# Row sums of squares by transposing and reducing instead of multiplying by ones, in a two-layer decoder trunk

## The chip, the cores and the metric

The kernel runs on one core of a Trainium2 chip. The metric is the time of one execution on the device in microseconds (us). Before the change it is 1353.64 us, the median of three runs (1351.68 to 1353.88).

A core has a matrix engine (TensorE, PE in the profile; its weight loads are listed apart as PEld), three engines for elementwise work (VectorE or DVE, ScalarE or ACT, GpSimd or POOL), and a queue engine that starts transfers (SyncE or SP). Matrix products are written to PSUM, which this kernel uses as eight banks of 128x512 float32 values; the other working memory is SBUF. Each engine has its own list of instructions and waits in it where an input or a buffer isn't ready.

## The reference

Two layers act on 512 tokens of width 1024, in float32. Layer 0 mixes tokens by four retention heads and four mLSTM heads, layer 1 by sparse attention. Each layer then has a gated MLP with a short convolution, and an embedding that is normed, gated and added. What matters here are the norms:

```python
def rms_norm(x, g):
    xf = x.astype(jnp.float32)
    y = xf * lax.rsqrt(jnp.mean(xf * xf, axis=-1, keepdims=True) + EPS)
    return (y * g.astype(jnp.float32)).astype(x.dtype)
...
    ret = rms_norm(ret, ret_g.reshape(R_HEADS, R_DV)).reshape(B, T, -1) * jax.nn.silu(rg)
...
    mlstm = jax.nn.sigmoid(mo) * rms_norm(hm, m_g.reshape(M_HEADS, M_DV)).reshape(B, T, -1)
```

Each needs, for every token, the sum of squares over the features. There are eight such norms over the full width (two mixers, two MLPs, two embeddings, two gates) and one for each of the eight heads of layer 0. The norms of queries and keys in layer 1 are computed in another way and aren't touched.

## The kernel before

The residual `h` lies transposed: eight tiles of 128 features by 512 tokens. Every float32 matrix is split into a high and a low part (`split`, L136 on ScalarE and L137 mostly on VectorE), and a product is made of three (`mm3`, L176 to L178): high by high, high by low, low by high. A weight tile is loaded by SyncE (`wr`), split into `wh` and `wl` with three buffers each, and used.

Since features lie along partitions, a sum over features has two steps. First, `acc_square` squares each of the eight tiles on ScalarE (L229, L232) and adds them up into one tile `acc` of 128x512 on GpSimd and VectorE (L234). Then `norm_sum` must add along the partitions and have one number for each token: for each of the four blocks `j` of 128 tokens it multiplies the block, as the stationary operand, by two columns of ones (L299). The result for 128 tokens stands in two equal columns of a PSUM bank, and L301 takes every second one and scales it. Tokens are now along partitions, four columns `v`. `rsqrt` (L215 to L221) gets the inverse root by three Newton steps on VectorE. `norm_cast` brings it back along the free axis with `spread`, which transposes four broadcast columns on TensorE (L307), and ScalarE copies that to `rb` (L312). `rb` multiplies what comes out of the products, so the products themselves don't wait for the norm.

In layer 0 the output `num` of each head is squared on ScalarE (`sq`, 128 features by 512 tokens), and `square_sums` (L510, L511) adds it up in the same manner into the columns `hd::4` of a 16-column tile, with a bank of kind "b" for each head.

PSUM banks are of three kinds, "a" (4), "b" (3) and "o" (1). `norm_sum` uses the "o" bank. The gate stage (`ple_gate`) runs its products through the four "a" banks; the first of them are freed only when L1592 has multiplied them by `rb`.

The order of the instructions on each engine is not the order of the source. A scheduler simulates the program with its own costs of instructions and writes the order out, so another form of the sums also moves other instructions.

Of the kernel before, what the change touches and what calls it, by code (L numbers as in the profile page):

```python
# [16 lines left out]
ALU = mybir.AluOpType  # L17
AX = mybir.AxisListType.X
PSUM = bass.MemoryType.PSUM

P = 128
T = 512
NTT = T // P
D = 1024
# [4 lines left out]
EPS = 1e-6  # L29
# [34 lines left out]
class Trunk:  # L64
# [226 lines left out]
    def norm_scale(self, n):  # L291
        self.norm_sum(n)
        self.norm_cast(n)

    def norm_sum(self, n):
        nc = self.nc
        ps = self.ps("o")
        for j in range(NTT):
            nc.tensor.matmul(ps[:, 2 * j : 2 * j + 2], n.acc[:, j * P : (j + 1) * P], self.ones[:, 0:2], start=True, stop=True)  # L299
        v = self.small(4)  # L300
        nc.vector.tensor_scalar(v, ps[:, 0:8:2], 1.0 / D, EPS, ALU.mult, ALU.add)  # L301
        n.r = self.rsqrt(v, 4)

    def spread(self, cols):
# [58 lines left out]
    def ab_mixer(self):  # L363
        nc, I, tc = self.nc, self.I, self.tc
        with ExitStack() as ctx:
# [84 lines left out]
            def ret_probs(banks):  # L450
                s = s_tile()
                for b, (c0, c1) in zip(banks, PARTS3):
                    self.split(s[:, 0, c0:c1], s[:, 1, c0:c1], b[:, 0 : c1 - c0])
                for i in range(NTT):
                    d = s[:, :, OFF[i] : OFF[i] + P]
                    nc.gpsimd.affine_select(d, d, pattern=[[0, 2], [1, P]], compare_op=ALU.is_ge, fill=0.0, base=0, channel_multiplier=-1)
                return s
# [16 lines left out]
            def lstm_probs(banks, e):  # L474
                main, rest = e
                s = s_tile()
                for b, (c0, c1) in zip(banks, PARTS3):
                    x = rest if c0 == 1024 else main[:, c0:c1]
                    nc.vector.tensor_tensor(x, b[:, 0 : c1 - c0], x, ALU.mult)
                    self.split(s[:, 0, c0:c1], s[:, 1, c0:c1], x)  # L480
                return s
# [23 lines left out]
                return sq  # L505

            def square_sums(hd, sq, ss):
                pss = self.ps("b")
                for j in range(NTT):
                    nc.tensor.matmul(pss[:, 2 * j : 2 * j + 2], sq[:, j * P : (j + 1) * P], self.ones[:, 0:2], start=True, stop=True)  # L510
                nc.vector.tensor_copy(ss[:, hd::4], pss[:, 0:8:2])  # L511


            def gate_sum(src):
# [49 lines left out]
            n = Norm()  # L564
# [42 lines left out]
            for idx in (0, 2, 1, 3):  # L607
                ps = pm[idx] if idx in pm else self.ws(I["w_mqk"][idx], n)
# [12 lines left out]
            def ret_out(hd, s, g):  # L621
                num = attend(hd, s, rv)
                gated(num, g, C_ABG + hd, ru[hd])
                return square(num)

            banks = pair_scores(rqk, 0, ("a", "b", "a"))
            ss = [ret_probs(b) for b in banks]
# [8 lines left out]
            sq = [ret_out(hd, ss[hd], gs[hd]) for hd in range(2)]  # L636
# [3 lines left out]
            ss = [ret_probs(b) for b in banks]  # L640
# [4 lines left out]
            for hd in range(2):  # L645
                square_sums(hd, sq[hd], rss)
            sq = [ret_out(2 + x, ss[x], g) for x, g in enumerate((g2, g3))]
# [6 lines left out]
            for hd in range(2):  # L654
                square_sums(2 + hd, sq[hd], rss)
# [18 lines left out]
            for c in range(2):  # L674
                self.cycle = ("b",)
                ro += [finish(ru, rr, 2 * c + x) for x in range(2)]
                gs = [gate_sum(I["w_mo"][2 * c])]

                with self.behind(nc.tensor):
                    banks = pair_scores(mqk, c, ("a", "a", "b"))  # L680
                ss = [lstm_probs(banks[0], es[2 * c])]
                nc.scalar.activation(gs[0], gs[0], AF.Sigmoid)
                ss.append(lstm_probs(banks[1], es[2 * c + 1]))
                gs.append(gate_tile(I["w_mo"][2 * c + 1], AF.Sigmoid))
                while mq:
                    square_sums(*mq.pop(0), mss)
                if c:
                    add_sums(0)
                both_sums = [key_sums(es[2 * c + x]) for x in range(2)]
                for x in range(2):  # L690
                    hd = 2 * c + x
                    num = attend(hd, ss[x], mv)
                    gated(num, gs[x], C_ABG + 4 + hd, mu[hd])
                    mq.append((hd, square(num)))
                sums = sums + both_sums if c else both_sums
# [1035 lines left out]
```

## Time and profile before

| | |
|---|---|
| three timed runs | 1351.68, 1353.64, 1353.88 us |
| the profiled execution | 1351.2 us, of which 1349.1 us from the first to the last instruction (the span) |
| TensorE | busy 1331.1 us, 99% of the span |
| VectorE | busy 1015.9 us, 75% |
| ScalarE | busy 735.7 us, 55% |
| GpSimd | busy 402.8 us, 30% |
| granted TensorE clock | 0.999 in the mean |

Times in the profile count from the start of the span. A row of the timeline has the start, the duration, the engine, the line, the operation, what it writes and reads, the shape and how many were merged; in brackets stands how long the engine was idle before it, and what ended that. Matrix products overlap their neighbours, so a row's duration is longer than the step from one start to the next. A row of the groups by line has the total busy time and the mean of one in ns, and then the idle time ahead of the group. The eight norm sums start at 31, 246, 470, 600, 646, 954, 1180 and 1310 us, the head sums stand in pairs at 108, 119, 170 and 180 us.

### The profile page before, as it was taken

To read this page: it belongs to the slowest core of one execution; us is meant where nothing else is said; L and a number is where in the kernel's file an instruction comes from. 1 tells how busy PE (TensorE), PEld (TensorE's weight loads), DVE (VectorE), ACT (ScalarE), POOL (GpSimd) and SP (SyncE) were. 2 spreads that over 40 slices of the span, in tenths; PEclk is the share of its full clock that TensorE was granted. 3 is DMA by queue.
4 is the path that set the end of the run, shared out by engine and by line. 5 is a ranking of instruction groups with operands and counts; after the bars stand their busy time and mean duration, and the time that the engine had idled before them with its cause. 6 is when DMAs were issued, how large, how long until landed. Compare 5 with 4: busy or idle time off the path is not lost. (4 is left out here: it accounts for less than half of the span.)

```text
span 1349.1 us, 21058 instructions
## 1 busy us (share of the span) xinstructions
PE 1331.1 (99%) x7782; PEld 1152.5 (85%) x7782; DVE 1015.9 (75%) x1638; ACT 735.7 (55%) x1301; POOL 402.8 (30%) x414
## 2 busy tenths in 40 slices
PE   9999999999999999999999999999999999999998
PEld 7888888888999999888788888888787999999887
DVE  6775867697888877678777878766797888877675
ACT  5357525454555555345466888674454555554342
POOL 3356432132111100331422887572232111110320
PEclk9999999999999999999999999999999999999999
DMA  6522355226666653433243231113225666653331
GB/s 239 161 98 94 110 141 182 88 90 179 166 174 176 167 132 91 129 113 118 82 156 110 82 95 52 32 52 98 90 90 172 167 174 174 167 135 90 133 96 63
DMA packets 68590, 167.23 MB, mean 124 GB/s; under 512 B 8068, under 2 KB 12804, under 8 KB 68488
## 3 DMA queue, kind: packets, MB, share of 16 engines
q1 hardware_dynamic: 59560, 150.02, 34.9%
q0 software_dynamic: 8640, 15.73, 7.0%
q8 instruction: 61, 1.00, 0.3%
q14 instruction: 41, 0.34, 0.1%
q10 hardware_dynamic: 288, 0.14, 0.0%
HBM read 146.71 MB, written 7.35 MB: 114 GB/s over the span
## 5 line engine op out<-in xcount | busy, mean ns | idle before, releaser
L136 ACT ACTIVATE wh<-wr 128x1024 fp32r<-128x1024 f32 (+2 forms) x186 | 190.7, 1028 | 216.6 <-PE ps L177 155.2
L137 DVE TENSOR_TENSOR wl<-wr,wh 128x1024 fp32r<-128x1024 f32 (+2 forms) x169 | 211.1, 1250 | 71.9 <-ACT wh L136 70.4
L176 PE MATMUL ps<-y,wh 128*128 128x512 f32 (+1 forms) x648 | 225.0, 351 | 1.0 <-ACT y L136 0.9
L177 PE MATMUL ps<-y,wh 128*128 128x512 f32 (+1 forms) x648 | 225.6, 349 | 0.0
L178 PE MATMUL ps<-y,wl 128*128 128x512 f32 (+1 forms) x648 | 224.2, 348 | 0.0
L176 PE MATMUL ps<-g,wh 128*128 128x512 f32 x380 | 148.3, 390 | 0.0
L177 PE MATMUL ps<-g,wh 128*128 128x512 f32 x380 | 148.3, 390 | 0.0
L178 PE MATMUL ps<-g,wl 128*128 128x512 f32 x380 | 148.0, 389 | 0.0
L176 PEld LDWEIGHTS ps<-y,wh 128*128 128x128 f32 x648 | 122.6, 189 | 18.4 <-ACT y L136 1.3
L177 PEld LDWEIGHTS ps<-y,wh 128*128 128x128 f32 x648 | 122.8, 190 | 15.6
L178 PEld LDWEIGHTS ps<-y,wl 128*128 128x128 f32 x648 | 122.8, 189 | 15.3
L234 POOL TENSOR_TENSOR acc<-acc,sc 128x512 f32<-128x512 f32 x36 | 58.1, 1615 | 128.6 <-ACT sc L232 127.6
L1437 POOL DMA_DIRECT2D es<-in_w_up_dram x30 | 26.3, 896 | 228.9 <-DVE sc L1397 107.9
L1078 POOL TENSOR_SCALAR pr<-pr,sm,gate 128x512 f32<-128x512 f32 (+3 forms) x128 | 77.0, 623 | 26.3 <-DVE sm L1076 21.6
L1503 DVE TENSOR_TENSOR hp<-hp,ps 128x512 f32<-128x512 f32 x96 | 65.3, 682 | 25.4 <-PE ps L178 25.4
L178 PEld LDWEIGHTS ps<-g,wl 128*128 128x128 f32 x380 | 71.4, 188 | 14.9
L176 PEld LDWEIGHTS ps<-g,wh 128*128 128x128 f32 x380 | 71.5, 188 | 14.0
L177 PEld LDWEIGHTS ps<-g,wh 128*128 128x128 f32 x380 | 71.5, 188 | 13.8
L1067 ACT ACTIVATE pr<-ps,nmx 128x512 f32<-128x512 f32 (+3 forms) x128 | 68.0, 539 | 12.8 <-DVE nmx L1065 6.9
L1430 POOL DMA_DIRECT2D ep<-ep x30 | 26.6, 912 | 160.7 <-DVE a L1475 51.2
L1470 ACT ACTIVATE sc<-ps 128x256 f32<-128x256 f32 x120 | 45.5, 379 | 52.4 <-PE ps L178 50.4
L176 PE MATMUL ps<-y,gh 128*128 128x256 f32 x240 | 68.5, 285 | 2.1 <-ACT sc L1470 2.1
(378 smaller groups left out, 3585.2 us busy)
## 6 DMA issues: line engine op xcount, KB each, us to landing
wr<-in_w_up_dram SPq DMA_DIRECT2D x58, 512.0 KB, 3.5
wr<-in_w_down_dram SPq DMA_DIRECT2D x64, 256.0 KB, 3.0
ep<-in_w_up_dram SPq DMA_DIRECT2D x30, 512.0 KB, 6.0
wr<-in_w_plg_dram SPq DMA_DIRECT2D x16, 512.0 KB, 3.5
es<-in_w_up_dram SPq DMA_DIRECT2D x30, 256.0 KB, 3.0
es<-in_w_up_dram POOLq DMA_DIRECT2D x30, 256.0 KB, 6.4
ep<-ep POOLq DMA_DIRECT2D x30, 256.0 KB, 3.6
wr<-in_w_down_dram SPq DMA_DIRECT2D x32, 192.0 KB, 2.5
```

The costliest lines, as they stand in the source:

```text
L136: self.nc.scalar.activation(hi, src, AF.Copy)
L137: (eng or self.nc.vector).tensor_tensor(lo, src, hi.bitcast(F32), ALU.subtract)
L176: mm(out, ah, bh, start=first, stop=False, **kw)
L177: mm(out, ah, bl, start=False, stop=False, **kw)
L178: mm(out, al, bh, start=False, stop=last, **kw)
L234: eng.tensor_tensor(n.acc, n.acc, sq, ALU.add)
L1067: nc.scalar.activation(pr[:, b], s[:, b], AF.Exp, bias=nmx[:, b : b + 1], accum_out=sm[:, bs[b] : bs[b] + 1])
L1078: nc.gpsimd.tensor_scalar(prs[b], prs[b], sm[:, b : b + 1], gate[:, j, hd, 1 + b : 2 + b], ALU.mult, ALU.mult)
L1430: nc.gpsimd.dma_start(me.two[:, :T], me.two[:, T:], accum_op=ALU.add)
L1437: nc.gpsimd.dma_start(me.s3, I["w_up"][i, me.f][:, :T], accum_op=ALU.add)
L1470: copy = lambda out, ps: nc.scalar.activation(out, ps, AF.Copy)
L1503: nc.vector.tensor_tensor(self.h[m], self.h[m], ps, ALU.add)
```

## The change

A new helper `token_sums` transposes the four blocks of 128x128 on TensorE into one bank, so that tokens are along partitions and features along the free axis, and VectorE adds up the 128 values of each block (`tensor_reduce` over the last axis, 128x512 to 128x4). `norm_sum` calls it, and then scales the four columns with an instruction of its own. `square_sums` calls it in place of products and copy.

```diff
+    def token_sums(self, out, src, ps):
+        for j in range(NTT):
+            self.nc.tensor.transpose(ps[:, j * P : (j + 1) * P], src[:, j * P : (j + 1) * P], self.ident)
+        self.nc.vector.tensor_reduce(out, ps.rearrange("p (j d) -> p j d", j=NTT), AX, ALU.add)
+
     def norm_sum(self, n):
         nc = self.nc
         ps = self.ps("o")
-        for j in range(NTT):
-            nc.tensor.matmul(ps[:, 2 * j : 2 * j + 2], n.acc[:, j * P : (j + 1) * P], self.ones[:, 0:2], start=True, stop=True)
         v = self.small(4)
-        nc.vector.tensor_scalar(v, ps[:, 0:8:2], 1.0 / D, EPS, ALU.mult, ALU.add)
+        self.token_sums(v, n.acc, ps)
+        nc.vector.tensor_scalar(v, v, 1.0 / D, EPS, ALU.mult, ALU.add)
         n.r = self.rsqrt(v, 4)
...
             def square_sums(hd, sq, ss):
-                pss = self.ps("b")
-                for j in range(NTT):
-                    nc.tensor.matmul(pss[:, 2 * j : 2 * j + 2], sq[:, j * P : (j + 1) * P], self.ones[:, 0:2], start=True, stop=True)
-                nc.vector.tensor_copy(ss[:, hd::4], pss[:, 0:8:2])
+                self.token_sums(ss[:, hd::4], sq, self.ps("b"))
```

In the order of the changed kernel, lines up to 293 keep their numbers, L301 becomes L305, `spread` is L311 and L312 becomes L316; lines behind `square_sums` move up by one.

VectorE at the norm of the first MLP, before (`acc` holds the squares, `ps` the sums, `wl` are low parts of weights):

```order
L234 TENSOR_TENSOR acc_2152<-acc_2152,sc_2194 128x512
L137 TENSOR_TENSOR wl_2332<-wr_2330,wh_2331 128x1024
L301 TENSOR_SCALAR tiny_2264<-ps_2259 128x4
L137 TENSOR_TENSOR wl_2403<-wr_2401,wh_2402 128x1024
L215 TENSOR_SCALAR tiny_2267<-tiny_2264 128x4
L216 TENSOR_SCALAR tiny_2266<-tiny_2267 128x4
```

and in the changed kernel:

```order
L234 TENSOR_TENSOR acc_2153<-acc_2153,sc_2195 128x512
L137 TENSOR_TENSOR wl_2334<-wr_2332,wh_2333 128x1024
L298 TENSOR_REDUCE tiny_2261<-ps_2260 128x4
L137 TENSOR_TENSOR wl_2405<-wr_2403,wh_2404 128x1024
L305 TENSOR_SCALAR tiny_2261<-tiny_2261 128x4
L215 TENSOR_SCALAR tiny_2269<-tiny_2261 128x4
L216 TENSOR_SCALAR tiny_2268<-tiny_2269 128x4
```

The reduction stands where the scaling stood, and the scaling now follows the weight split; nothing else moved there.

TensorE in the gate stage of layer 0, before, from the spread (L307) to the first product of the next output bank (`ps_5973`; the products of L176 to L178 for one bank are 24):

```order
L307 MATMUL ps_5876<-ident,tiny_5862 128x128 x4
L177 MATMUL ps_5936<-y_5764,wh_5930 128x512
L178 MATMUL ps_5936<-y_5763,wl_5931 128x512
L176 MATMUL ps_5936<-y_5770,wh_5930 128x512
L177 MATMUL ps_5936<-y_5771,wh_5930 128x512
L178 MATMUL ps_5936<-y_5770,wl_5931 128x512
L176 MATMUL ps_5936<-y_5777,wh_5930 128x512
L177 MATMUL ps_5936<-y_5778,wh_5930 128x512
L178 MATMUL ps_5936<-y_5777,wl_5931 128x512
L176 MATMUL ps_5936<-y_5784,wh_5930 128x512
L177 MATMUL ps_5936<-y_5785,wh_5930 128x512
L178 MATMUL ps_5936<-y_5784,wl_5931 128x512
```

and in the changed kernel (`ps_5977` is the next bank):

```order
L178 MATMUL ps_5940<-y_5773,wl_5935 128x512
L311 MATMUL ps_5880<-ident,tiny_5866 128x128 x4
L176 MATMUL ps_5940<-y_5780,wh_5934 128x512
L177 MATMUL ps_5940<-y_5781,wh_5934 128x512
L178 MATMUL ps_5940<-y_5780,wl_5935 128x512
L176 MATMUL ps_5940<-y_5787,wh_5934 128x512
L177 MATMUL ps_5940<-y_5788,wh_5934 128x512
L178 MATMUL ps_5940<-y_5787,wl_5935 128x512
L176 MATMUL ps_5977<-y_5739,wh_5971 128x512
```

The spread moved back by five products: 6 of them now lie between it and the next bank, where there were 11. The last gate stage has the same move, the first norm moves its spread by four products and the layer-1 mixer by three.

ScalarE at the start of the layer-1 mixer, before (`wh` are high parts of weights, `rb` the spread norm):

```order
L136 ACTIVATE wh_6380<-wr_6379 128x1024
L136 ACTIVATE wh_6427<-wr_6426 128x1024
L312 ACTIVATE rb_6307<-ps_6308 128x512
L136 ACTIVATE wh_6458<-wr_6457 128x1024
L199 ACTIVATE sc_6340<-ps_6323 64x512
```

and in the changed kernel:

```order
L136 ACTIVATE wh_6385<-wr_6384 128x1024
L136 ACTIVATE wh_6432<-wr_6431 128x1024
L136 ACTIVATE wh_6463<-wr_6462 128x1024
L316 ACTIVATE rb_6312<-ps_6313 128x512
L199 ACTIVATE sc_6345<-ps_6328 64x512
```

One more weight copy now stands ahead of `rb`. On VectorE the split of that weight moved ahead of the first work with `rb` in the same way.

## The prediction

> **What bounds the kernel now.** I read the page's busy shares and slices first, then TensorE's waits, then single stretches of the timeline around the operations that change.
>
> ```profile
> PE 1331.1 (99%) x7782; PEld 1152.5 (85%) x7782; DVE 1015.9 (75%) x1638; ACT 735.7 (55%) x1301; POOL 402.8 (30%) x414
> ...
> PE   9999999999999999999999999999999999999998
> ```
>
> TensorE (PE) works through 99% of the 1349.1 us and is full in every slice. VectorE (DVE) has a quarter of the span free on average. So the first question for each edit is whether it shortens PE's own instruction stream, and the second is where PE already waits, since a gain ahead of such a wait is lost in it.
>
> ```profile
> PE ps L176 <- ACT wh L136: 2.9, 3, 1.2
> ...
> PE ps L177 <- DVE wl L137: 1.5, 1, 1.5
> ...
> PE ps L299 <- DVE acc L234: 0.8, 1, 0.8
> ```
>
> These are the longest of PE's waits for ScalarE and for VectorE, and the only one at a line that changes (us in total, times, longest). They are short, and none is a wait for a sum; the last is a sum that waits for its input.
>
> **PE: what is removed and added.** Sixteen groups change: eight norm sums (L299) and eight head sums (L510), each of four 128-column blocks.
>
> ```profile
> L299 PE MATMUL ps<-ones,acc x64: 164/251/252, 31.1 to 1310.6; 128*128 128x2 f32 x64
> ...
> L510 PE MATMUL ps<-ones,sc x64: 164/251/252, 108.5 to 181.7; 128*128 128x2 f32 x64
> ...
> L307 PE MATMUL ps<-ident,tiny x64: 271/273/289, 40.7 to 1319.5; 128*128 128x128 f32 x64
> ...
> L988 PE MATMUL ps<-ident,y x64: 272/273/298, 717.5 to 835.5; 128*128 128x128 f32 x64
> ```
>
> L299 issues 8 x 4 = 32 products and leaves 64 records: a product of float32 with the ones is two passes, each with a weight load, however few columns it has. L307, the helper `spread`, issues 16 x 4 = 64 transposes and leaves 64 records, and so does L988 (16 heads x 4), whose input is ordinary data as in the change. So the records fall from 128 to 64. The records overlap, so I take the cost of a group from the starts of its neighbours, the neighbours' own steps (0.23 us each) taken off:
>
> ```profile
> 246.19 0.39 PE L178 MATMUL ps<-g,wl 128*128 128x512 f32 x1
> 246.42 0.95 PE L299 MATMUL ps<-ones,acc 128*128 128x2 f32 x8
> 247.23 0.49 PE L176 MATMUL ps<-fh,wh 128*128 128x512 f32 x1
> 247.55 0.40 PE L177 MATMUL ps<-fh,wh 128*128 128x512 f32 x1
> ...
> 252.59 0.39 PE L178 MATMUL ps<-g,wl 128*128 128x512 f32 x1
> 252.81 0.60 PE L307 MATMUL ps<-ident,tiny 128*128 128x128 f32 x4
> 253.17 0.48 PE L176 MATMUL ps<-fh,wh 128*128 128x512 f32 x1
> 253.48 0.39 PE L177 MATMUL ps<-fh,wh 128*128 128x512 f32 x1
> ```
>
> A norm sum: 247.55 - 246.19 - 2 x 0.23 = 0.90 us. Four transposes: 253.48 - 252.59 - 0.46 = 0.43, say 0.44. Two head sums one after the other:
>
> ```profile
> 108.32 0.39 PE L177 MATMUL ps<-s,v 128*128 128x512 f32 x1
> 108.55 1.84 PE L510 MATMUL ps<-ones,sc 128*128 128x2 f32 x16
> 110.25 0.48 PE L178 MATMUL ps<-s,v 128*128 128x512 f32 x1
> 110.56 0.33 PE L176 MATMUL ps<-s,v 128*128 128x384 f32 x1
> ```
>
> 110.56 - 108.32 - 0.46 = 1.78, so 0.89 each. PE's stream gets shorter by 0.46 us a group, 16 x 0.46 = 7.3 us in all. [...]
>
> **DVE: what is added.** Each head's copy of 128x4 becomes a reduction of 128x512 in PSUM. Each norm gets such a reduction and keeps its scale-and-add.
>
> ```profile
> L301 DVE TENSOR_SCALAR tiny<-ps 128x4 f32<-128x4 f32 x8 | 1.3, 162 | 3.2 <-PE ps L299 3.2
> ...
> L511 DVE COPY tiny<-ps 128x4 f32<-128x4 f32 x8 | 1.1, 155 | 8.3 <-PE ps L510 8.3
> ```
> ```profile
> L1065 DVE TENSOR_REDUCE nmx<-ps 128x1 f32<-128x512 f32 x32 | 21.9, 686 | 6.4 <-PE ps L1064 6.3
> L1065 DVE TENSOR_REDUCE nmx<-ps 128x1 f32<-128x384 f32 x32 | 17.4, 551 | 1.6 <-PE ps L1064 1.2
> ```
>
> L1065 is a reduction of the same 128x512 in PSUM, to one maximum; a sum to four columns is not in the trace, and I take 0.69 us; ends are 0.55 (the narrower form) and 1.2 (the 128x512 turned out to cost as much as one 128x1024 pass, L137, does in rows quoted below). Heads: 8 x (0.69 - 0.16) = 4.2 us. Norms: 8 x 0.69 = 5.5. DVE does 9.7 us more. It stood idle 8.3 us just ahead of these copies, waiting for PE, so the 4.2 us fit there; PE needs the heads' factors only after the steps of `rsqrt`. At the upper end, 1.2 us, the heads would take 8.3 and still fit. In a norm the chain sum, Newton steps, spread gets longer by 0.69, less 0.35 by which the fourth transpose ends sooner (0.60 against 0.95 us after the first start). The tightest spread is that of the MLP norm:
>
> ```profile
> 250.65 0.16 DVE L221 SCALAR_TENSOR_TENSOR tiny<-tiny,tiny 128x4 f32<-128x4 f32 x1
> ```
>
> The last step ends at 250.81 and its spread starts at 252.81, quoted above: 2.0 us of cover. The spread comes 0.46 sooner, the chain ends 0.34 later, so 1.2 us remain. Without this cover each of the norms would pay its lateness on PE.
>
> **Where the gain is kept, and where not.** From the start to the layer-1 mixer PE hardly waits, so the 11 groups up to 470 us (three norms, eight heads) should keep 11 x 0.46 = 5.0 us. The two waits for weights inside each MLP are released by chains that begin with PE itself (weights split after their buffers come free), so they move along. In the layer-1 mixer it is different:
>
> ```profile
> 635.65 9.64 POOL L234 TENSOR_TENSOR acc<-acc,sc 128x512 f32<-128x512 f32 x6 [38.78 <-ACT sc L232]
> ```
> ```profile
> 646.16 1.02 PE L299 MATMUL ps<-ones,acc 128*128 128x2 f32 x8 [0.79 <-DVE acc L234]
> ```
> ```profile
> 656.03 1.06 ACT L136 ACTIVATE wh<-wr 128x1024 fp32r<-128x1024 f32 x1 [9.30 <-PE ps L193]
> 657.00 0.58 ACT L312 ACTIVATE rb<-ps 128x512 f32<-128x512 f32 x1
> ```
> ```profile
> 668.38 0.68 DVE L788 TENSOR_TENSOR sc<-sc,rb 48x512 f32<-48x512 f32 x1
> 668.99 1.21 DVE L137 TENSOR_TENSOR wl<-wr,wh 128x1024 fp32r<-128x1024 f32 x1
> ```
> ```profile
> 670.25 0.50 PE L177 MATMUL ps<-wl,y 128*128 128x512 f32 x1 [1.54 <-DVE wl L137]
> ```
>
> The norm sum at 646 waits for squares that GpSimd has added up for 9.64 us, and GpSimd's start hangs on the gate of the step before. A PE that arrives 0.46 sooner (the group at 600) waits 0.46 longer. The same holds for the group at 646 itself: at 670 PE waits for a weight split that stands behind `rb` and L788 in DVE's order. The new order puts the spread three products later there (+0.68 us, less 0.46) and one 1.06 us weight copy ahead of `rb` on ScalarE, but moves the matching weight split on DVE ahead too. I charge +0.25 for the stage, with -0.8 and +1.1 as ends (the copy comes for free, or all of it lands on the wait). Both groups bring nothing: 0 instead of 0.92, and -0.25.
>
> The other move is in the two gate norms (600 and 1310). The spread now stands 6 products ahead of the next output bank instead of 11, and that bank is freed by the first L1592 behind `rb`:
>
> ```profile
> 609.61 0.60 PE L307 MATMUL ps<-ident,tiny 128*128 128x128 f32 x4
> ...
> 610.87 1.89 DVE L1592 TENSOR_TENSOR sc<-ps,rb 128x512 f32<-128x512 f32 x3 [1.92 <-ACT rb L312]
> ```
>
> L1592 ends its first third at 611.50, 1.89 us after the spread's start. Six products and four transposes last 6 x 0.23 + 0.44 = 1.82. So PE now waits about 0.1 to 0.3 us there; before it had 1 us to spare. At 600 this disappears in the wait at 646; at 1310 it costs 0.2. The groups at 954, 1180 and 1310 keep 3 x 0.46 = 1.4.
>
> The queue of SyncE has head-gate weights moved ahead of the rotary copies at 45 to 65 us and the order of two loads changed near 200 us; PE reads none of it within several us, so I set 0 (it would show as a new wait of PE on `wl` or `hp`, at most about the 1 us of its present waits). GpSimd's order is unchanged.
>
> Sum: 5.0 + 0 - 0.25 + 1.4 - 0.2 = 5.9 us. The profiled execution took 1351.2 us (span 1349.1 and 2.1 around it), hence 1345.3. It is 0.5 us below the fastest of the three timed runs and 2.4 below their median of 1353.64, from which I get 1347.7. I say 1347.5.
>
> **Rivals.**
> Part of the gain is lost to new waits. The instructions stand in another order on PE, DVE and ScalarE in three stages, and a few waits of 1 us (the size of those quoted) would leave 2 to 3 us: 1351. For it: the stage at 600 to 670 is tight on DVE. Against: only norms' surroundings are reordered. 0.10.
>
> The change does not do what it says on PE: transposes of data take two passes, as the products do. Then PE gains nothing, 1353.6. Against it: 64 records for 64 calls in L307 and L988. 0.02.
>
> Slower by VectorE: the reductions stand in series with PE, at each norm's spread and each head's bank. Then 9.7 us of DVE less 7.3 of PE, 1356.0. The point from which it decides is the 2.0 us of cover at 250.81; the chain would have to grow by three times what I work out. 0.03.
>
> [...]
>
> ```profile
> 747.00:920.00 173.00, 172.82 (x1237) 145.60 (x1236) 129.92 (x303) 134.56 (x389) 126.94 (x173) 1.00 0.21 58
> 950.00:1025.00 75.00, 72.86 (x318) 59.26 (x317) 65.77 (x102) 36.58 (x51) 15.83 (x10) 0.98 0.27 86
> 1021.00:1025.50 4.50, 4.50 (x13) 3.56 (x14) 4.50 (x6) 0.93 (x2) 1.09 (x1) 0.62 0.35 117
> ```
>
> The third column from the end is the granted clock: 0.62 over 4.5 us, that is 1.7 us lost (4.5 x 0.38). [...] 0.02. [...]
>
> **How the numbers follow.** Faster with the gain mostly kept has 0.83: from 1351.2 - 7.3 = 1343.9 (nothing lost, runs as fast as the profiled one) up to 1350. With the part-lost case the range is 1343.9 to 1351.4. A measurement can tell about 0.2%, 2.7 us, from no change; the part-lost case lies on this edge and goes two thirds to "same". Faster 0.86, same 0.10, slower 0.04, the last from the two slow rivals in part (1356.0 is itself near the edge).
>
> **What would show it.** Right: PE has 7718 records, four to a sum, 0.44 us a group; a new DVE group of 16 reductions near 0.69 us; the span about 6 us shorter, 5 of them already there at 500 us; the wait at 646 longer by about 0.5; a short wait of PE behind the spread near 612 and 1320. Wrong: eight records to a sum; PE waiting on `tiny` or for a spread; reductions over 1 us; new waits of PE for weights before 300 us; more stretches with a clock below 1.

## The result, and the profile after

The changed kernel takes 1345.32 us in the median of six runs (1344.20 to 1346.86), the kernel before 1353.76 us in the median of six on the same chip (1351.68 to 1354.40). The ratio is 0.9942 with an interval of 0.9931 to 0.9952, so the change is worth about 0.6%. The profiled execution took 1344.21 us with a span of 1342.5 us, 6.6 us less than before's span.

The page of after, the lines that answer to those of before (busy us, share of the span, instructions; then TensorE's tenths in 40 slices):

```profile
PE 1324.4 (99%) x7718; PEld 1144.4 (85%) x7718; DVE 1024.1 (76%) x1646; ACT 736.0 (55%) x1301; POOL 403.9 (30%) x414
...
PE   9999999999999999999999999999999999999998
```

TensorE has 64 records less (7718) and is still full in every slice. VectorE is busy 8.2 us longer in 8 more instructions (the rows' durations add up to 10.0 us more; where they overlap, the busy time counts them once). So the bound has not moved, its stream got shorter. Line numbers behind the change are a little higher in this kernel: transposes L297, reduction L298, `spread` L311, `rb` L316, and one more than before from L788 on.

TensorE's waits in after (who waits for what: us in total, times, longest):

```profile
PE ps L176 <- ACT wh L136: 3.2, 3, 1.2
PE ps L176 <- ACT sc L1471: 2.5, 2, 1.7
PE ps L178 <- DVE wl L137: 2.2, 3, 1.0
...
PE ps L297 <- DVE acc L234: 1.0, 1, 1.0
...
PE ps L796 <- ACT sc L790: 0.7, 1, 0.7
```

The list has no wait for a reduction or for a factor that comes from one; a short one at the banks of the gate, which is not listed, is shown further down. The wait of 1.5 us at L177 that stood in before is gone, and a new, shorter one has appeared at L796.

The new line of VectorE in after's trace (count, then shortest, median and longest in ns):

```profile
L298 DVE TENSOR_REDUCE tiny<-ps x16: 676/688/694, 32.0 to 1304.3; 128x4 f32<-128x512 f32 x16
...
  PE ps L297: 14.1, 6
```

The sixteen reductions take 0.688 us each. The second line is VectorE's idle time just ahead of them, waiting for the transposes: 14.1 us, more than the 11.0 us they last.

TensorE's timeline in after, at the same three places as shown of before:

```profile
108.13 0.39 PE L177 MATMUL ps<-s,v 128*128 128x512 f32 x1
108.36 1.03 PE L297 MATMUL ps<-ident,sc 128*128 128x128 f32 x8
109.15 0.47 PE L178 MATMUL ps<-s,v 128*128 128x512 f32 x1
109.47 0.33 PE L176 MATMUL ps<-s,v 128*128 128x384 f32 x1
...
242.53 0.39 PE L178 MATMUL ps<-g,wl 128*128 128x512 f32 x1
242.76 0.60 PE L297 MATMUL ps<-ident,acc 128*128 128x128 f32 x4
243.11 0.48 PE L176 MATMUL ps<-fh,wh 128*128 128x512 f32 x1
243.43 0.40 PE L177 MATMUL ps<-fh,wh 128*128 128x512 f32 x1
...
248.69 0.60 PE L311 MATMUL ps<-ident,tiny 128*128 128x128 f32 x4
```

From neighbour to neighbour, two steps of 0.23 us taken off, two head sums cost 109.47 - 108.13 - 0.46 = 0.88 us (1.78 before), and the norm sum 243.43 - 242.53 - 0.46 = 0.44 us (0.90 before).

**Where the 6.6 us came from.** I compared the start of the same TensorE product in the two timelines. After is ahead by:

| before's time, us | ahead, us | what happened since the row above |
|---|---|---|
| 247 | 4.1 | ten groups, 0.44 each, less 0.3 lost in the first microseconds |
| 318 | 2.5 | 1.6 lost: half the clock in after alone |
| 346 | 1.9 | a longer wait at the start of the embedding stage (1.72 against 1.10 us) |
| 601 | 2.8 | two groups |
| 646 | 2.2 | gate's bank wait 0.3, and 0.25 more wait for `acc` |
| 664 | 2.7 | the group at 646 |
| 680 | 3.8 | the layer-1 mixer's gate: another order |
| 955 | 4.3 | one group |
| 1026 | 5.6 | 1.6 won: half the clock in before alone; 0.3 lost in a longer wait for `wh` |
| 1311 | 6.9 | two groups, and 0.4 around the second embedding stage |
| end | 6.6 | gate's bank wait 0.3 |

### The profile page after: what moved, and what is told of

It is laid out like the page before. It is cut to its first block, busy times and chain, and to the rows that moved or that the text cites. A ratio compares the mean times of both kernels' runs of the same rounds, so it can differ in the third digit from the quotient of the medians.

```text
span 1342.5 us, 20941 instructions
## 1 busy us (share of the span) xinstructions
PE 1324.4 (99%) x7718; PEld 1144.4 (85%) x7718; DVE 1024.1 (76%) x1646; ACT 736.0 (55%) x1301; POOL 403.9 (30%) x414
## 5 line engine op out<-in xcount | busy, mean ns | idle before, releaser
L176 PE MATMUL ps<-y,wh 128*128 128x512 f32 (+1 forms) x648 | 225.4, 352 | 0.9 <-ACT y L136 0.9
L177 PE MATMUL ps<-y,wh 128*128 128x512 f32 (+1 forms) x648 | 225.3, 348 | 0.0
L178 PE MATMUL ps<-y,wl 128*128 128x512 f32 (+1 forms) x648 | 223.9, 348 | 0.0
L176 PE MATMUL ps<-g,wh 128*128 128x512 f32 x380 | 148.2, 390 | 0.0
L177 PE MATMUL ps<-g,wh 128*128 128x512 f32 x380 | 148.2, 390 | 0.0
L178 PE MATMUL ps<-g,wl 128*128 128x512 f32 x380 | 147.8, 389 | 0.0
L176 PEld LDWEIGHTS ps<-y,wh 128*128 128x128 f32 x648 | 122.8, 190 | 19.0 <-ACT y L136 1.3
L177 PEld LDWEIGHTS ps<-y,wh 128*128 128x128 f32 x648 | 122.7, 189 | 15.5
L178 PEld LDWEIGHTS ps<-y,wl 128*128 128x128 f32 x648 | 122.6, 189 | 15.4
L178 PEld LDWEIGHTS ps<-g,wl 128*128 128x128 f32 x380 | 71.4, 188 | 15.0
L176 PEld LDWEIGHTS ps<-g,wh 128*128 128x128 f32 x380 | 71.5, 188 | 14.0
L177 PEld LDWEIGHTS ps<-g,wh 128*128 128x128 f32 x380 | 71.5, 188 | 13.8
L1471 ACT ACTIVATE sc<-ps 128x256 f32<-128x256 f32 x120 | 45.5, 379 | 51.2 <-PE ps L178 49.3
L176 PE MATMUL ps<-y,gh 128*128 128x256 f32 x240 | 68.3, 285 | 2.5 <-ACT sc L1471 2.5
```

The lines of the kernel that those rows point to most:

```text
L176: mm(out, ah, bh, start=first, stop=False, **kw)
L177: mm(out, ah, bl, start=False, stop=False, **kw)
L178: mm(out, al, bh, start=False, stop=last, **kw)
L1471: copy = lambda out, ps: nc.scalar.activation(out, ps, AF.Copy)
```

## The experiments

Where a profiled execution is named below, the first thing to know is how often TensorE's clock was halved in it (the last section shows it). Each such stretch lasts 3.4 us and costs about 1.6 us. In that form the spans compare better: before 1349.1 with one stretch, after 1342.5 with one.

**Each half of the change alone.** The first keeps the new form for the norms, the second for the heads; the other half is as before.

```diff
 # e1_norms_only
-                self.token_sums(ss[:, hd::4], sq, self.ps("b"))
+                pss = self.ps("b")
+                for j in range(NTT):
+                    nc.tensor.matmul(pss[:, 2 * j : 2 * j + 2], sq[:, j * P : (j + 1) * P], self.ones[:, 0:2], start=True, stop=True)
+                nc.vector.tensor_copy(ss[:, hd::4], pss[:, 0:8:2])
 # e2_heads_only
+        for j in range(NTT):
+            nc.tensor.matmul(ps[:, 2 * j : 2 * j + 2], n.acc[:, j * P : (j + 1) * P], self.ones[:, 0:2], start=True, stop=True)
         v = self.small(4)
-        self.token_sums(v, n.acc, ps)
-        nc.vector.tensor_scalar(v, v, 1.0 / D, EPS, ALU.mult, ALU.add)
+        nc.vector.tensor_scalar(v, ps[:, 0:8:2], 1.0 / D, EPS, ALU.mult, ALU.add)
```

> Only the eight norm sums go through transposes and reductions; the head sums stay products with ones. Theory (TensorE's own stream is what counts, 0.46 us less for each group): 8 x 0.46 = 3.7 us less than before, less up to 0.9 for the two gate norms that wait for an output bank, plus what the new order in the layer-1 mixer gave (about 1 us): 3 to 4.5 us less, about 1350. Rival (VectorE's added work is on the path): 3.7 less 5.5 of reductions, 1 to 2 us slower than before. Rival (the heads carry the whole gain): within 1 us of before.

> Only the eight head sums change; the norms stay products with ones. Theory: 8 x 0.455 = 3.6 us less than before, all of it kept, since no wait of TensorE lies near the heads and the order elsewhere stays that of before; about 1350. The two parts alone should add up to the whole (6.6 in the spans, 8 in the timed runs) within 1.5 us. Rival (VectorE's added 4.2 us is on the path): 0.6 us slower than before.

Norms alone: 1348.52 us against 1353.08 us, ratio 0.9959 (0.9947 to 0.9971). Heads alone: 1348.73 us, ratio 0.9961 (0.9947 to 0.9974). Each half is worth about 0.4%: 5.5 us (3.9 to 7.2) and 5.3 us (3.5 to 7.2), more than the 3 to 4.5 and the 3.6 us I expected. Together they would make 0.8%, some 3 us more than the whole change with its 0.58% (0.48 to 0.69), where I had allowed 1.5 us; the intervals are too wide to say that the halves do not add up. Neither rival holds: both halves are faster than before. The profiled execution of the second had two stretches of half clock and a span of 1349.1 us, equal to before's: from that one execution alone the heads would have seemed to bring nothing.

**The cost on TensorE, doubled.** Every transpose is issued twice into the same place.

```diff
 # e3_transposes_twice
-            self.nc.tensor.transpose(ps[:, j * P : (j + 1) * P], src[:, j * P : (j + 1) * P], self.ident)
+            for _ in range(2):
+                self.nc.tensor.transpose(ps[:, j * P : (j + 1) * P], src[:, j * P : (j + 1) * P], self.ident)
```

> The changed kernel with every transpose of the sums issued twice into the same place, 64 more on TensorE, nothing more on VectorE. Theory: 64 x 0.11 = 7.0 us more than the changed kernel, so within 1.5 us of the kernel before, and eight records to a sum. Rival (the gain came from the new order of instructions, not from the shorter stream): 1 to 2 us more than the changed kernel, still 5 us or more below before.

1353.22 us against 1353.08 us, ratio 0.9995 (0.9982 to 1.0007): the gain is gone. The groups by line in this kernel (busy us, mean ns, then idle time ahead):

```profile
L299 DVE TENSOR_REDUCE tiny<-ps 128x4 f32<-128x512 f32 x16 | 10.8, 687 | 11.1 <-PE ps L298 10.8
...
L298 PE MATMUL ps<-ident,acc 128*128 128x128 f32 x64 | 8.3, 273 | 1.0 <-DVE acc L234 1.0
...
L298 PE MATMUL ps<-ident,sc 128*128 128x128 f32 x64 | 8.0, 272 | 0.0
```

Here there are 128 records in the sums, as many as before's products had, in the new form and with VectorE's new work. The time is before's time. So the gain is in the main TensorE's shorter stream, not VectorE's part and not the new order by itself.

**The cost on VectorE, doubled.**

```diff
 # e4_reduce_twice
-        self.nc.vector.tensor_reduce(out, ps.rearrange("p (j d) -> p j d", j=NTT), AX, ALU.add)
+        for _ in range(2):
+            self.nc.vector.tensor_reduce(out, ps.rearrange("p (j d) -> p j d", j=NTT), AX, ALU.add)
```

> The changed kernel with each reduction issued twice, 16 x 0.69 = 11 us more on VectorE, nothing more on TensorE. Theory (VectorE has cover at all sums but those of the two gate norms, where the next output bank waits for the spread): 0.7 us more at each gate norm, perhaps 0.7 in the layer-1 mixer, so 1.5 to 2.5 us more than the changed kernel and 5 to 6.5 below before. Rival (the reductions are in series with TensorE): 11 us more than the changed kernel, 3 to 4 above before.

1349.68 us against 1353.08 us, ratio 0.9969 (0.9957 to 0.9981). That is 0.27% more than after (whose interval ends at 0.9952, below this one), some 3.7 us for 11 us of added VectorE work: more than the 1.5 to 2.5 us I expected, a third of what work in series would cost. The groups by line, and TensorE's waits in this kernel:

```profile
L299 DVE TENSOR_REDUCE tiny<-ps 128x4 f32<-128x512 f32 x32 | 21.0, 682 | 10.6 <-PE ps L297 10.6
```
```profile
PE ps L177 <- DVE wl L137: 2.1, 1, 2.1
...
PE ps L176 <- DVE sc L1594: 1.4, 2, 0.7
```

Compared product by product with after, nothing is lost at the eight heads and at the first three norms. Each gate norm loses 0.68 us, as expected, and there TensorE now waits for L1594 (L1592 in before, which frees the gate's banks): the second line, twice. The layer-1 mixer loses 1.6 us, where 0.7 was expected, besides another 1.6 us of a stretch of half clock that fell on it, and the wait for the split weights (first line) is back at 2.1 us. Each MLP loses 0.6 us, which I had not expected: 50 us behind the norm TensorE waits for a weight split at a place where no other kernel here waits.

```profile
297.59 0.50 PE L178 MATMUL ps<-fh,wl 128*128 128x512 f32 x1 [0.49 <-DVE wl L137]
...
1008.81 0.50 PE L178 MATMUL ps<-fh,wl 128*128 128x512 f32 x1 [0.75 <-DVE wl L137]
```

The split that it waits for took 2.32 us on VectorE both times, against 1.21 us for the one at this place in after. The orders of the mixer and of the MLPs were written anew for this kernel, so these terms are not the price of the reduction alone.

**The layer-1 mixer.** After, with the old products in this one norm.

```diff
 # e5_mixer1_old
     def norm_sum(self, n, old=False):
...
+        if old:
+            for j in range(NTT):
+                nc.tensor.matmul(ps[:, 2 * j : 2 * j + 2], n.acc[:, j * P : (j + 1) * P], self.ones[:, 0:2], start=True, stop=True)
+            nc.vector.tensor_scalar(v, ps[:, 0:8:2], 1.0 / D, EPS, ALU.mult, ALU.add)
+        else:
...
-                self.norm_scale(n)
+                self.norm_scale(n, True)
```

> The changed kernel, with the old products of ones at one place alone, the norm of the layer-1 mixer (646 us before). Theory: the change brought 1.3 us or so between 645 and 680 us, of which 0.46 from the shorter sum and the rest from the order that the scheduler wrote there (the gate's transposes of L795 now stand in front of the wait for a weight split instead of behind it). Taking the edit out there should bring the old order and the old wait of 1.5 us back: 1 to 1.5 us more than the changed kernel. Rival (the gain there is only the sum): 0.5 us more.

1346.57 us against 1352.39 us, ratio 0.9956 (0.9944 to 0.9968); after itself, beside it on the same chip, had 0.9941 (0.9928 to 0.9955). In the totals the two intervals overlap, so the stage must be read in the timeline. From 642 to 680 us this kernel loses 3.1 us against after, 1.6 of it in a stretch of half clock, so 1.5 us are the stage's, as expected: 0.5 us for the longer sum and 1.0 for the order. TensorE's timeline in it:

```profile
665.86 1.07 PE L176 MATMUL ps<-wh,y 128*128 128x512 f32 x4
668.47 0.50 PE L177 MATMUL ps<-wl,y 128*128 128x512 f32 x1 [1.54 <-DVE wl L137]
```

With the old sum the old order comes back, and with it the wait of 1.54 us. The same place in after:

```profile
664.91 1.07 PE L176 MATMUL ps<-wh,y 128*128 128x512 f32 x4
666.72 0.45 PE L796 MATMUL ps<-ident,sc 48*128 48x48 f32 x4 [0.74 <-ACT sc L790]
667.10 0.50 PE L177 MATMUL ps<-wl,y 128*128 128x512 f32 x1
```

After does four transposes of the mixer's gate (L796) in what was the wait, and the product behind them starts 2.19 us after the group of four before it, 2.61 in the kernel with the old sum. In before they stood between products, where they cost their full time:

```profile
676.72 0.28 PE L870 MATMUL ps<-wh,pt 128*128 128x256 f32 x1
676.93 0.44 PE L795 MATMUL ps<-ident,sc 48*128 48x48 f32 x4
677.30 0.73 PE L176 MATMUL ps<-wh,y 128*128 128x512 f32 x2
```

**Is it the transposes, or the passes?** Before's kernel, with sums and ones in `float32r`, the type in which `split` holds the high parts. The squares, or their sum in a norm, have no low part here, so what a low part would hold is left out.

```diff
 # e6_one_pass, against the kernel before
+        self.ones2 = self.const.tile([P, 2], F32R, name="ones2")
...
+                out = n.sum = self.scp.tile([P, T], F32R, name=self.nm("sc"), tag="sc")
...
-            nc.tensor.matmul(ps[:, 2 * j : 2 * j + 2], n.acc[:, j * P : (j + 1) * P], self.ones[:, 0:2], start=True, stop=True)
+            nc.tensor.matmul(ps[:, 2 * j : 2 * j + 2], n.sum[:, j * P : (j + 1) * P], self.ones2, start=True, stop=True)
...
-                sq = self.sc()
+                sq = self.scp.tile([P, T], F32R, name=self.nm("sc"), tag="sc")
...
-                    nc.tensor.matmul(pss[:, 2 * j : 2 * j + 2], sq[:, j * P : (j + 1) * P], self.ones[:, 0:2], start=True, stop=True)
+                    nc.tensor.matmul(pss[:, 2 * j : 2 * j + 2], sq[:, j * P : (j + 1) * P], self.ones2, start=True, stop=True)
```

> The kernel before, with the products of two columns of ones kept, but the squares and the ones written as float32r, so that each product is one pass; the squares lose low bits. VectorE has none of the added work. Theory (a pass costs TensorE 0.11 us, whatever it is): four records to a sum as with transposes, TensorE's stream the same 7.3 us shorter; less VectorE work, so no wait at the output banks of the gate norms (0.3 and 0.6 in the changed kernel); 0 to 1.5 us less than the changed kernel, about 1344.5. Rival (the gain is a property of transposes): 2 us or less below before.

1345.14 us against 1352.39 us, ratio 0.9944 (0.9932 to 0.9957), the same gain without a transpose and without VectorE's reduction. A norm sum in its timeline (L304 is before's L299):

```profile
242.58 0.39 PE L180 MATMUL ps<-g,wl 128*128 128x512 f32 x1
242.81 0.50 PE L304 MATMUL ps<-ones,sc 128*128 128x2 f32 x4
243.17 0.49 PE L178 MATMUL ps<-fh,wh 128*128 128x512 f32 x1
243.50 0.40 PE L179 MATMUL ps<-fh,wh 128*128 128x512 f32 x1
```

Four records instead of eight, and 243.50 - 242.58 - 0.46 = 0.46 us: a pass costs 0.11 us whether it is a transpose of 128 columns or a product with two. What the change removes is the second pass. That this kernel would be up to 1.5 us below the changed one can't be told from the runs: after itself had 1343.85 us beside it.

**After once more, and other banks for the gates.** The first is the changed kernel unaltered; the second lets the gate stage use the three "b" banks too, so that no product waits there for a bank behind the spread; the third joins those banks with the one-pass sums.

```diff
 # e8_gate_banks (and, with the edit of e6, e9_one_pass_banks)
         n = self.norm_in(C_PLG + 8 * i)
+        self.cycle = ("a", "b")
...
                         finish(*wait.pop(0))
+        self.cycle = ("a",)
```

> The changed kernel once more, unaltered, beside the others. Theory: stretches of 3.4 us at half the clock come at other places or in other numbers in another execution of the same program, each worth about 1.6 us, and make the steps of 1 to 2 us between the timed runs; about 1345.3 again, ratio 0.993 to 0.996. Rival (the stretches belong to the order of instructions): one stretch again, near 310 us.

> The changed kernel, with the products of the two gate stages going in turn through the a and the b banks (7 instead of 4). Theory: TensorE's wait behind the spread of the two gate norms, 0.3 us near 608 and 0.6 near 1315, goes; the second is worth 0.6 in the end, the first disappears in the wait at 646; 0.3 to 1 us less than the changed kernel. Rival (the wait there is not for a bank): no change within 0.3 us and the same wait.

> Both variants together: products of ones in one pass of float32r in place of transposes and reductions, and the gate stages over seven banks. Theory: TensorE's stream as short as in the changed kernel, 9.7 us less on VectorE, no bank wait; since both gave nothing that could be told from the changed kernel alone, at most 1.5 us below it: ratio to before 0.992 to 0.995. Rival (the small gains add up to something that shows): below 0.992.

After again: 1343.85 us against 1352.39 us, ratio 0.9941 (0.9928 to 0.9955), the same as the first time. Its profiled execution had a span of 1347.1 us, 4.6 us more than the first profile of the same program: one more stretch of half clock (at 1019 us, beside the one near 309 us), and longer waits of TensorE (4.6 us instead of 2.5 for the `sc` of L1471, and 1.0 us for a `pr` of GpSimd). That such stretches make the steps between the timed runs is not borne out. One stretch alone lowers the mean clock to 0.9987, so an execution listed with 1.0 has none; seven of before's, beside the halves, have 1.0 and still range from 1350.21 to 1353.62 us. Beside after again, its five executions with 1.0 took 1343.55 to 1343.94 us and before's two 1351.56 and 1351.74: without any stretch the change is worth 7.9 us, by no more than two executions of before. Gate banks: 1344.37 us, ratio 0.9933 (0.9919 to 0.9947). The two longer steps behind the spread are gone from its timeline at both gates, 0.3 us each (not 0.6 at the last one, as I had expected), but the total can't be told from after's. Both together: 1343.76 us against 1351.59 us, ratio 0.9948 (0.9935 to 0.9960). No version was clearly faster than the change.

## Why the prediction was right, and where it was not

The time and the range held, and the mechanism is the one forecast: a shorter TensorE stream, with VectorE's new work beside it. Step by step:

- **TensorE, 0.46 us a group.** Right: 0.90 to 0.44 us, four records a sum, 7718 records. Doubling the transposes took the gain away. The one-pass products, four records and 0.46 us a sum, say why the factor is two here: one pass against two.
- **The reduction, 0.69 us.** Right: 0.688 us, the same as the reduction of that size to one maximum. The upper end of 1.2 us wasn't needed: before's trace has sums of 128x512 to several columns too, at L942 to 128x8 in 0.686 us.
- **The cover.** Right, to the tenth. VectorE's timeline in after shows the last step of the MLP norm:

```profile
247.32 0.16 DVE L221 SCALAR_TENSOR_TENSOR tiny<-tiny,tiny 128x4 f32<-128x4 f32 x1
```

  It ends at 247.48 us and its spread starts at 248.69 us (shown above): 1.2 us are left, as worked out. With reductions twice as long nothing is lost at this spread.
- **The bank wait behind the gates' spreads.** Right in place, slightly low in size. TensorE's timeline in after:

```profile
609.29 0.40 PE L177 MATMUL ps<-y,wh 128*128 128x512 f32 x1
609.52 0.40 PE L178 MATMUL ps<-y,wl 128*128 128x512 f32 x1
609.94 0.50 PE L176 MATMUL ps<-y,wh 128*128 128x512 f32 x1
610.28 0.40 PE L177 MATMUL ps<-y,wh 128*128 128x512 f32 x1
```

  Two steps of 0.42 and 0.34 instead of 0.23: 0.30 us, where 0.2 was charged. It is too short to be listed as a wait; with longer reductions the list names it (L1594). As forecast, the gain of the group at 600 vanished: 0.3 us in this bank wait and 0.25 in the wait for `acc` (0.79 to 1.04 us, where 0.5 more was forecast).
- **The waits for weights in the MLPs.** Right in the first, where they stayed at 0.85 and 0.99 us. In the second the one for `wh` grew from 0.85 to 1.14 us (1.13 in the second profile of after), a loss of 0.3 us that the sum didn't have.
- **The layer-1 mixer, a loss of 0.25 us.** Wrong, and the only step that failed in kind. Between 600 and 680 us, groups included, after went from 2.3 us ahead (the group at 600 not yet counted) to 3.8: a gain of 1.5 us instead of a loss of 0.25, outside the ends I had given. I followed `rb`, the weight copy and the split to the wait at 670 and asked when that wait would end. I did not ask what TensorE could do meanwhile: the new order puts the gate's four transposes into the wait, and the split itself starts 3.2 us earlier (665.83 us against 668.99), 0.4 more than the 2.7 us that after was ahead by then. Restoring the old sum in this one norm brought both the wait and 1.5 us back, 0.5 of it the sum itself.
- **"5 of them already there at 500 us."** Wrong in this profile: 2.3 us. The eleven groups did give their 0.44 each. But 0.3 us went in the first microseconds, 1.6 in a stretch of half clock and 0.6 in the wait at 346 us; the last two differ between executions of one program. A milestone of a few us, read from one execution of each kernel, was set finer than such a comparison can hold.
- **The clock.** That the added transposes would slow the kernel through it, for which 0.02 was kept, is not borne out: with 64 more of them the time was before's, and no stretch began at a sum's transposes. Before and the two kernels with one-pass sums have none of the new transposes; before and one of those two show a stretch all the same. The count did differ by execution (one to three with the transposes, none or one without), so a small effect on how often it happens is not excluded; the last section shows what went ahead of the stretches in before and after.
- **From 5.9 us to the median.** The span fell by 6.6 us, and the runs' ratio stands for 6.5 to 9.3 us, so the gain was larger than the 5.9 us. That the sum came so near is in part luck. Up to 600 us after won 2.3 us (5.0 forecast), from there to 680 us 1.5 (-0.25), up to 1311 us 3.1 (1.4), and at the end it lost 0.3 (0.2). One stretch of half clock in each of the two profiles cancels (1.6 us lost in the first part, won in the third), and the 1.75 us by which the mixer was better than forecast stand in for the small losses elsewhere that the sum didn't have. The median is 2.2 us below the forecast of 1347.5: 0.7 for the span, 0.4 for the time around it (1.7 us instead of 2.1), and 1.3 because after's median lies 1.1 us above its profiled execution where 2.4 was added, less 0.2 by rounding. Why before's lies 2.4 us above is open.

## What to carry to other kernels

When one engine is full, count its passes as well as its columns: here a pass cost 0.11 us with 2 columns as with 128 (0.23 with 512), and a product of float32 with two columns of ones paid two, so a one-pass form (a transpose with the sum on another engine, or a one-pass type where its precision is enough) halved it. Work moved to another engine is free only where a measured cover stands, and the size of that cover can be read ahead of time as the distance between the end of the chain and the start of its user. Where a scheduler writes a new order, ask of each wait not only when it will end but what may be put into it, and compare stages over more than one profiled execution before explaining a microsecond.

## What the runs showed of the hardware

**A clock that halves now and then, for 3.41 us.** The windows view of before, then of after, for the same two places (the third column from the end is the granted clock):

```profile
305.00:315.00 10.00, 8.16 (x35) 6.15 (x34) 9.95 (x16) 5.36 (x8) 2.18 (x1) 1.00 0.20 59
...
1016.00:1027.00 11.00, 9.16 (x32) 6.80 (x31) 9.57 (x15) 4.29 (x6) 2.18 (x1) 0.84 0.22 71
```
```profile
305.00:315.00 10.00, 8.16 (x28) 5.94 (x27) 8.58 (x13) 4.29 (x6) 2.17 (x1) 0.83 0.25 79
...
1016.00:1027.00 11.00, 10.05 (x44) 8.35 (x45) 10.14 (x13) 5.36 (x7) 2.04 (x1) 1.00 0.43 135
```

Before has it in the second MLP, after in the first: 10 us at 0.83 are 1.7 us lost. (In the comparison of products the stretch costs about 1.6 us.) The second profile of after's program has it in both:

```profile
305.00:315.00 10.00, 8.16 (x28) 5.99 (x27) 8.33 (x13) 4.29 (x6) 2.17 (x1) 0.83 0.28 86
1014.00:1026.00 12.00, 9.88 (x36) 7.33 (x35) 9.62 (x15) 5.41 (x8) 2.18 (x1) 0.86 0.24 76
```

TensorE's timeline of after at the first place shows what goes ahead:

```profile
307.29 0.50 PE L176 MATMUL ps<-fh,wh 128*128 128x512 f32 x1 [0.85 <-ACT wh L136]
...
309.01 0.51 PE L178 MATMUL ps<-fh,wl 128*128 128x512 f32 x1 [0.99 <-DVE wl L137]
...
310.34 0.63 PE L176 MATMUL ps<-gh,wh 128*128 128x512 f32 x1
310.77 0.63 PE L177 MATMUL ps<-gh,wh 128*128 128x512 f32 x1
```

Two waits within 2.6 us, then products at a step of 0.43 instead of 0.23 us. Before has the same two waits of 0.85 and 0.99 us at its first MLP and keeps the full clock there (1.00 in its row at 305), so the length of the waits alone does not decide it. In both traces the granted clock is 0.50 for 3.413 us and then full again: from 1021.72 us in before and from 309.69 in after.

In before the record of the granted clock starts at 4.55 us and the half clock comes 1017.17 us later, in after at 5.91 us and 303.79 us later: 298 and 89 times 3.413 us, to 0.1 us. Here are steps of that length, counted from the start of the stretch: the two around the waits of before's first MLP and the one ahead of its stretch, then the one ahead of after's stretch (the second number is TensorE's busy time):

```profile
308.33:311.74 3.41, 2.56 (x11) 1.80 (x10) 3.41 (x7) 1.96 (x3) 0.00 (x0) 1.00 0.00 0
311.74:315.15 3.41, 2.42 (x11) 1.68 (x10) 3.41 (x5) 1.70 (x3) 2.18 (x1) 1.00 0.32 78
1018.31:1021.72 3.41, 1.57 (x6) 0.94 (x6) 3.41 (x6) 2.99 (x4) 1.81 (x1) 1.00 0.00 0
```
```profile
306.28:309.69 3.41, 1.57 (x6) 0.89 (x6) 3.41 (x6) 3.04 (x5) 1.76 (x1) 1.00 0.00 0
```

Where the full clock stays, the two waits fall into two steps (0.85 and 0.99 us without a product); where it is lost, both fall into one, with 1.84 us in either trace. From the start of the record to the step with the last product, the next longest time without one, 1.43 us in a step of before (666.73 us) and in one of after (1012.84 us), was followed by full clock. So the same waits came before a stretch in one place and not in the other, and they lay differently in this count. That this decides it is not shown: no run moved the waits against the count. And the time without a product is not the whole of it: in the kernel with the old sum in the layer-1 mixer a wait of 1.04 us at 642.79 us stood ahead of a stretch (products at a step of 0.43 us from 645.21 us), where after's wait of 1.04 us at the same place did not (0.23 us from 645.33 us).

**One wait, several lengths.** The wait of TensorE for the `sc` of L1471, at the start of the first embedding stage, was 1.72 us in one execution of after and 2.10 in another. What sets it was not tried.
